# A two-layer attention trunk in one core: the identity matrix made by GpSimd instead of loaded, and a new order of instructions

## The chip, the core and the metric

The kernel runs on one core of a Trainium2 chip. The core has a TensorE for matmuls (PE in the profile, its weight loads PEld), a VectorE (DVE), a ScalarE (ACT), a GpSimd (POOL) and a SyncE (SP); transfers are issued here by SP and by ScalarE and carried out by 16 DMA engines. The metric is the device time of one execution in microseconds. Before the change it is 305.41 us (median of three runs, 304.03 to 306.15).

## The reference

A sequence of 256 tokens of width 1024 passes through two layers. Each layer normalises x, applies a shift and a scale that come from a conditioning vector c, runs its attention mixer, and adds the result to x through a gate from c. A last normalisation follows. Cut to what matters:

```python
c_act = silu(c)
for layer in range(2):
    shift, scale, gate = split(c_act @ w_ada[layer] + b_ada[layer], 3)
    h = rms_norm(x, norm_g[layer]) * (1 + scale) + shift
    if layer == 0:   # projection 1024 -> 2840, two head groups:
        # A: 8 query heads on 1 key head, window 128, with a sink per head
        # B: 8 query heads on 2 key heads: compressed keys, selected blocks and a window, gated
        y = even_mixer(h, w_in_even, w_out_even, ...)
    else:            # projection 1024 -> 4096, 16 heads, blocks of 256 keys
        y = odd_mixer(h, w_in_odd, w_out_odd, ...)
    x = x + gate * y
return rms_norm(x, final_g)

# compressed keys and values of B: windows of 32 tokens every 16, as one row each
k_cmp = gelu((windows(k) + pe_k) @ w1_k) @ w2_k      # w1: 2048 x 256
```

All of it is in float32. The attention outputs are multiplied by the silu of a part of the projection before the output projection.

## The kernel before

**Planned order.** The kernel's Python code first records every operation (class Plan, record) with what it depends on; then Plan.issue (line 262) makes the real calls in the order of a table of about 2900 numbers, ORDER. All operations therefore carry the line of that call, L269, in the profile, and are told apart by their tiles. Each engine executes its own operations in this order, one behind the other: an operation that has to wait holds back all that stands behind it on its engine. The same goes for the DMAs that SP or ScalarE issues. A second table, FLIP, names the copies, scalings and affine maps that go to the other one of ScalarE and DVE than the code says.

**Arithmetic.** A float32 product is made of three matmuls (mm3): high part by high part, high by low, low by high. Weights arrive in one of five raw buffers of 1 MB each (raw0 to raw4); ScalarE casts them to the high part whi, DVE subtracts to get the low part wlo. hhi and hlo are the same two parts of the layer's input h, transposed; ghi and glo those of the attention's output.

**The opening.** TensorE begins with filler matmuls on a constant matrix ones, whose results are not used (into ps_m and ps_o). ScalarE's queue loads norm_g and b_ada (into rows), the table tbl_a (into ta, 128 x 160: columns 0 to 127 the identity matrix ident, 128 to 159 a selection matrix sel) and c (into crow, 8 x 128). SP's queue loads x (two halves of 128 tokens, xs), the first weights of w_in_even (raw) and those of w_ada. small_c transposes crow on TensorE with ident into ps_pt, and makes silu(c) from it (ACT tiny, DVE tiny, DVE cz). For each half of x, ScalarE squares and sums (ACT t<-xs), GpSimd takes the inverse root (r, with a power by expo), DVE and ScalarE scale (t<-xs,r), TensorE transposes (ps_s<-ta,t and ps_pj<-ta,t), and copies bring the result to xT, which lies in bigA.

**Shift and scale of layer 0.** They are made for groups of the eight row blocks g of the weights: START says for one block, then two, two, two and one. For each group, w_ada lands in tiles that are used later for other things (qT, gate, oT, kTb, t, called room in start_ada), and start_sums multiplies with cz on TensorE (ps_m<-qT,cz, ps_m<-oT,cz, ...) and partly on DVE (acc). blk and asb fold the sums, shs holds the result, and start_prep makes hhi and hlo of block g by ScalarE and DVE. start_mm then adds block g to seven accumulators.

**After that** follow rotary embeddings, transposes and attention A, the compression (compress_mlp: weights cmp_w1_k and cmp_w1_v in raw buffers, multiplied directly, ps_m<-raw,t), attention B, the output projection (ps_s<-whi,ghi), and the change of layer: out of the sums of squares in parts comes the inverse root, t<-xs,parts scales, TensorE transposes, t<-ps_pj,shs applies scale and shift, hhi and hlo are made, and the second layer's projection begins (ps_pj<-whi,hhi). The second layer's shift, scale and gates are made on DVE along the way (acc<-raw,cz,acc, summed over partitions by a matmul with ones). The last product is normalised and stored.

Transposes everywhere multiply by ident. sel has two readers: the compression, and selbc, a copy of one column of sel that GpSimd spreads over 128 columns.

## Time and profile before

| what | value |
|---|---|
| runs, median | 305.41 us (304.03, 305.41, 306.15) |
| the profiled execution | 303.29 us |
| its span, first to last instruction | 301.4 us |
| TensorE busy | 290.8 us (96%) |
| DVE busy | 258.1 us (86%) |
| ScalarE busy | 198.5 us (66%) |
| GpSimd busy | 11.4 us (4%) |
| DMA | 71.83 MB, mean 238 GB/s |

The profile shows one execution on the chip. Times of its rows are microseconds from the start of the span. A row of the timeline has start, length, engine, line, operation, output and inputs; in brackets stands the idle time of the engine before it and what ended that. Matmul ends are modelled, so the distance between the starts of two matmuls says more of their price than their length does. A wait for several things is put down to the one that came last by the profile. What the profiled execution takes outside its span is 303.29 - 301.4 = 1.9 us.

### The profile page before, as it was taken

The numbers are of one execution on the slowest core, as the hardware profiler recorded it, in microseconds if no ns is written. First come the engines' busy times: TensorE is split into PE (matmuls) and PEld (weight loads), VectorE is DVE, ScalarE is ACT, GpSimd is POOL, SyncE is SP. The second block draws the span as 40 slices with busy tenths as digits, with TensorE's granted clock in tenths as the row PEclk, the third lists the DMA queues.
The fourth block names the chain that finished last, engine by engine and source line by source line (L and its number), as shares of the span: only waits on it lengthen the run. The fifth ranks groups of instructions, "written<-read, shape, count | busy, mean of one in ns | idle before, by whom it ended". The sixth has DMA issues, their size and how long they took to land.

```text
span 301.4 us, 6166 instructions
## 1 busy us (share of the span) xinstructions
PE 290.8 (96%) x2268; PEld 250.4 (83%) x2268; DVE 258.1 (86%) x648; ACT 198.5 (66%) x506; POOL 11.4 (4%) x36
## 2 busy tenths in 40 slices
PE   7999999999999999999998999999999999999990
PEld 6888888897698888777877799999889989887890
DVE  0479988999999999999999867998788999987873
ACT  1655646796999989996459764377376467782620
POOL 1300000002000000000010000000000000000021
PEclk9999999999999999999999999999999999999998
DMA  7999999975989774389995947099782973103103
GB/s 244 368 385 369 397 350 377 385 240 170 377 265 340 266 256 157 113 285 372 292 299 186 315 134 272 4 306 383 222 255 93 311 246 100 44 3 138 71 2 139
DMA packets 60751, 71.83 MB, mean 238 GB/s; under 512 B 2761, under 2 KB 52401, under 8 KB 60721
## 3 DMA queue, kind: packets, MB, share of 16 engines
q1 hardware_dynamic: 60176, 70.92, 69.1%
q10 hardware_dynamic: 544, 0.51, 0.5%
q8 instruction: 18, 0.29, 0.4%
q14 instruction: 13, 0.10, 0.1%
HBM read 70.38 MB, written 1.05 MB: 237 GB/s over the span
## 4 chain that ended last, share of the span: by engine, by line
PE 89%; DVE 3%; ACT 2%; issue 2%; DMA 2%; POOL 1%; ACTq 0%; POOLq 0%; DVEq 0%
PE ps_pj L269 56%; PE ps_s L269 10%; PE ps_pt L269 8%; PE ps_o L269 8%; PE ps_m L269 7%; DMA crow<-in_c_dram 2%; DVE t L269 1%; ACT t L269 1%; DVE xs L269 1%; ACT whi L269 1%; ACTq L269 0%; POOL parts L269 0%; DVE acc L269 0%; DVE wlo L269 0%; POOLq L1393 0%
## 5 line engine op out<-in xcount | busy, mean ns | idle before, releaser
L269 ACT CAST whi<-raw 128x512 fp32r<-128x512 f32 (+2 forms) x108 | 72.0, 691 | 32.3 <-PE ps_pj L269 17.9
L269 PE MATMUL ps_pj<-hhi,whi 128*128 128x256 f32 x256 | 74.0, 296 | 0.0
L269 PE MATMUL ps_pj<-hlo,whi 128*128 128x256 f32 x256 | 72.8, 290 | 0.0
L269 DVE TENSOR_TENSOR wlo<-raw,whi 128x512 fp32r<-128x512 f32 (+2 forms) x92 | 70.8, 792 | 2.2 <-ACT whi L269 1.9
L269 PE MATMUL ps_pj<-hhi,wlo 128*128 128x256 f32 x256 | 70.7, 287 | 0.0
L269 PEld LDWEIGHTS ps_pj<-hhi,whi 128*128 128x128 f32 x256 | 47.8, 188 | 2.8 <-issue 2.0
L269 PEld LDWEIGHTS ps_pj<-hlo,whi 128*128 128x128 f32 x256 | 47.9, 188 | 1.9 <-issue 1.7
L269 PEld LDWEIGHTS ps_pj<-hhi,wlo 128*128 128x128 f32 x256 | 47.3, 188 | 0.7 <-issue 0.6
L269 DVE SCALAR_TENSOR_TENSOR acc<-raw,cz,acc 128x512 f32<-128x512 f32 x56 | 41.6, 744 | 0.3
L269 ACT ACTIVATE sm<-sm,mn 128x256 f32<-128x256 f32 (+1 forms) x58 | 26.0, 450 | 7.3 <-DVE mn L269 7.3
L269 PE MATMUL ps_pj<-whi,hhi 128*128 128x512 f32 (+2 forms) x72 | 25.8, 377 | 0.5 <-ACT hhi L269 0.5
L269 PE MATMUL ps_pj<-wlo,hhi 128*128 128x512 f32 (+2 forms) x72 | 25.9, 377 | 0.0
L269 PE MATMUL ps_pj<-whi,hlo 128*128 128x512 f32 (+2 forms) x72 | 25.3, 372 | 0.0
L269 DVE SCALAR_TENSOR_TENSOR wlo<-raw,whi 128x512 fp32r<-128x512 f32 x32 | 21.2, 686 | 3.7 <-ACT whi L269 3.6
L269 PE MATMUL ps_pj<-wlo,ghi 128*128 128x512 f32 (+1 forms) x56 | 20.6, 371 | 0.0
L269 PE MATMUL ps_pj<-whi,glo 128*128 128x512 f32 (+1 forms) x56 | 20.6, 370 | 0.0
L269 PE MATMUL ps_pj<-whi,ghi 128*128 128x512 f32 (+1 forms) x56 | 20.5, 368 | 0.0
L269 ACT ACTIVATE sm<-sm,rc 128x256 f32<-128x256 f32 (+1 forms) x44 | 18.7, 453 | 2.0 <-DVE rc L269 2.0
L269 PE MATMUL ps_pt<-ta,sm 128*128 128x128 f32 x87 | 17.8, 274 | 0.0
L269 DVE TENSOR_TENSOR t<-ps_pj,tb 128x512 f32<-128x512 f32 (+2 forms) x22 | 12.1, 588 | 4.4 <-PE ps_pj L269 4.4
L269 PEld LDWEIGHTS ps_pj<-whi,hhi 128*128 128x128 f32 x72 | 13.4, 188 | 2.8 <-ACT hhi L269 1.2
L269 ACT ACTIVATE whi<-raw 128x512 fp32r<-128x512 f32 x16 | 9.7, 627 | 8.8 <-PE ps_pj L269 5.3
(241 smaller groups left out, 610.1 us busy)
## 6 DMA issues: line engine op xcount, KB each, us to landing
raw<-in_w_ada_dram SPq DMA_DIRECT2D x32, 512.0 KB, 5.0
raw<-in_w_in_odd_dram SPq DMA_DIRECT2D x16, 1024.0 KB, 7.0
raw<-in_w_in_even_dram SPq DMA_DIRECT2D x8, 652.0 KB, 7.0
raw<-in_w_in_even_dram SPq DMA_DIRECT2D x5, 1024.0 KB, 7.0
raw<-in_w_out_even_dram SPq DMA_DIRECT2D x4, 1024.0 KB, 5.2
raw<-in_w_out_odd_dram SPq DMA_DIRECT2D x4, 1024.0 KB, 6.5
qT<-in_w_ada_dram SPq DMA_DIRECT2D x12, 256.0 KB, 6.2
t<-in_w_ada_dram SPq DMA_DIRECT2D x8, 256.0 KB, 6.5
```

Of the source, the lines that this page charges most:

```text
L269: self.ops.append(dict(key=eng.key, deps=deps, fn=lambda: getattr(real, name)(*args, **kw)))
```

## The change

The table tbl_a shrinks to 128 x 32, the selection matrix alone. It is loaded by SP behind the tables of the rotary embedding. ident is a tile of its own, which GpSimd fills with ones and then cuts to the diagonal, as its first work in the kernel. The copy selbc goes, as do functions that no call reached with the settings of before (ada_tile, ada_rows) and the settings themselves (SS_ON, G0_ON, G1_ON); the matmuls stay the same in number and shape. Both tables, ORDER and FLIP, are new.

```diff
-    ta = const([P, 160], "ta")
+    ident = const([P, P], "ident")
+    sel = const([P, 32], "sel")
+    G.memset(ident, 1.0)
+    G.affine_select(out=ident, in_=ident, compare_op=ALU.is_equal, fill=0.0, base=0, pattern=[[-1, P]], channel_multiplier=1)
...
-    A.dma_start(ta, tbl_a)
...
-    ident = ta[:, 0:128]
-    sel = ta[:, 128:160]
...
-    selbc = const([P, P], "selbc")
-    G.tensor_copy(selbc, sel[:, 0:1].to_broadcast([P, P]))
...
     Y.dma_start(tb, tbl_b[:, :1056])
+    Y.dma_start(sel, tbl_a)
...
-    a = np.zeros((P, 160), np.float32)
-    a[:, :128] = np.eye(P)
+    a = np.zeros((P, 32), np.float32)
...
-            a[32 * q + m, 128 + m] = 1.0
+            a[32 * q + m, m] = 1.0
...
 ORDER = [int(i) for i in """
-93 4 5 3 6 0 8 20 21 22 23 24 25 26 27 28 29 50 54 55 56 57 30 58 31 32 33 34 35 53 1 62 59 97 2 52 1010 1015 40
+7 0 2 4 1 9 21 22 23 24 25 26 27 28 29 30 54 31 32 33 34 6 3 41 5 93 97 96 92 94 55 95 77 56 100 98 62 78 79 35
...
```

By FLIP, DVE now makes more of the opening's copies to bigA (and fewer of asb), and in the attention stage fewer copies of kTb and scalings of sm and more of the copies pT; the count of ScalarE's operations is the same.

GpSimd's instructions begin, behind four small constants, with the memset of ident, a reload of its library, the select, then the memset of expo and the root r; the memset of cz (288 columns), which was the first, stands behind the roots. The library reload stood between the memset of expo and the first operation of r before.

In the opening, this is ScalarE's instruction stream before (tiny is the silu of c; t_88 and t_90 take the squares of the two halves of x):

```order
L269 DMA rows<-in_norm_g_dram 16x128
L269 DMA rows<-in_b_ada_dram 48x128
L269 DMA ta<-in_tbl_a_dram 128x160
L269 DMA crow<-in_c_dram 8x128
L269 ACT_TABLE_LOAD
L269 ACTIVATE tiny_86<-ps_pt_85 128x8
L269 ACTIVATE t_88,r_87<-xs 128x1024
L269 CAST whi_110<-raw_101 128x152
```

And after:

```order
L266 DMA crow<-in_c_dram 8x128
L266 DMA rows<-in_b_ada_dram 48x128
L266 DMA rows<-in_norm_g_dram 16x128
L266 ACT_TABLE_LOAD
L266 ACTIVATE tiny_86<-ps_pt_85 128x8
L266 ACTIVATE t_90,r_87<-xs 128x1024
L266 ACTIVATE t_88,r_87<-xs 128x1024
L266 CAST whi_109<-raw_101 128x512
L266 CAST whi_110<-raw_101 128x512
```

The load of crow has moved from the last of ScalarE's four to the first of its three, that of ta is gone, and the two squares follow each other without a cast between.

On TensorE, these rows lead to the first projection matmul of the opening before (they follow the sums ps_m<-qT,cz; ps_m<-oT,cz are the same kind of sums for the next two row blocks; whi and hhi belong to the projection; x8 counts like rows in a run):

```order
L269 MATMUL ps_pj_95<-ta,t_91 128x128 x2
L269 MATMUL ps_s_93<-ta,t_89 128x128 x2
L269 MATMUL ps_pj_95<-ta,t_91 128x128
L269 MATMUL ps_pj_94<-ta,t_91 128x128
L269 MATMUL ps_m_67<-blk,asb_107 128x2
L269 MATMUL ps_o_69<-ones 128x128
L269 MATMUL ps_s_93<-ta,t_89 128x128
L269 MATMUL ps_o_69<-ones 128x128
L269 MATMUL ps_pj_95<-ta,t_91 128x128
L269 MATMUL ps_m_67<-oT,cz 32x128 x8
L269 MATMUL ps_pj_96<-whi_109,hhi 128x512
```

And after:

```order
L266 MATMUL ps_pj_95<-ident,t_91 128x128
L266 MATMUL ps_pj_94<-ident,t_91 128x128
L266 MATMUL ps_pj_95<-ident,t_91 128x128 x2
L266 MATMUL ps_pj_94<-ident,t_91 128x128
L266 MATMUL ps_m_68<-blk,asb_107 128x2
L266 MATMUL ps_s_93<-ident,t_89 128x128 x2
L266 MATMUL ps_o_70<-ones 128x128
L266 MATMUL ps_pj_95<-ident,t_91 128x128
L266 MATMUL ps_o_70<-ones 128x128 x2
L266 MATMUL ps_s_93<-ident,t_89 128x128
L266 MATMUL ps_pj_96<-whi_109,hhi 128x512
```

The eight matmuls ps_m<-oT,cz no longer stand ahead of the first projection matmul (ps_pj_96<-whi_109,hhi); they come behind 13 matmuls of the projection. On SP, the two loads of xs are now the first two DMAs; before, they were the second and the fourth, with tiles of w_ada and of w_in_even ahead of them.

At the change of layer, TensorE's stream before is (ps_s<-whi,ghi is the output projection of layer 0, ps_pj_96 and ps_o the transposes of the first tokens, ps_pj_94 the projection of layer 1):

```order
L269 MATMUL ps_s_93<-whi_110,ghi 128x512
L269 MATMUL ps_s_93<-wlo_114,ghi 128x512
L269 MATMUL ps_s_93<-whi_110,glo 128x512
L269 MATMUL ps_pj_96<-ta,t_88 128x128 x4
L269 MATMUL ps_o_69<-ta,t_88 128x128 x4
L269 MATMUL ps_pj_94<-whi_111,hhi 128x512
L269 MATMUL ps_pj_94<-wlo_115,hhi 128x512
L269 MATMUL ps_pj_94<-whi_111,hlo 128x512
```

And after:

```order
L266 MATMUL ps_s_93<-whi_110,glo 128x512
L266 MATMUL ps_pj_96<-ident,t_88 128x128 x3
L266 MATMUL ps_s_93<-whi_110,ghi 128x512
L266 MATMUL ps_pj_96<-ident,t_88 128x128
L266 MATMUL ps_s_93<-wlo_114,ghi 128x512
L266 MATMUL ps_s_93<-whi_110,glo 128x512
L266 MATMUL ps_o_70<-ident,t_88 128x128 x3
L266 MATMUL ps_pj_94<-whi_111,hhi 128x512
L266 MATMUL ps_pj_94<-wlo_115,hhi 128x512
L266 MATMUL ps_o_70<-ident,t_88 128x128
L266 MATMUL ps_pj_94<-whi_111,hlo 128x512
```

Three matmuls of the output projection now stand between the transposes of ps_pj_96 and those of ps_o, and the first two matmuls of the next projection ahead of the last transpose. On ScalarE, the cast that stood between the two t<-xs,parts has moved away from there.

For the compression, SP's stream before holds these loads (raw_101 to raw_105 are raw0 to raw4; cmp_w_k and cmp_w_v with 128x8x256 are the 1 MB weights):

```order
L269 DMA tb<-in_tbl_b_dram 128x1056
L269 DMA raw_104<-in_w_in_even_dram 128x8x256
L269 DMA raw_101<-in_w_in_even_dram 128x8x256
L269 DMA raw_105<-in_w_in_even_dram 128x8x256
L269 DMA raw_102<-in_cmp_w_k_dram 128x8x256
L269 DMA raw_103<-in_cmp_w_k_dram 128x8x256
L269 DMA raw_104<-in_cmp_w_v_dram 128x8x256
L269 DMA w2v<-in_cmp_w_v_dram 128x2x64
L269 DMA raw_105<-in_cmp_w_v_dram 128x8x256
L269 DMA raw_102<-in_w_in_even_dram 128x8x256
L269 DMA w2k<-in_cmp_w_k_dram 128x2x64
```

And after:

```order
L266 DMA tb<-in_tbl_b_dram 128x1056
L266 DMA raw_105<-in_w_in_even_dram 128x8x256
L266 DMA snk<-in_a_sinks_dram 128x8
L266 DMA w2v<-in_cmp_w_v_dram 128x2x64
L266 DMA w2k<-in_cmp_w_k_dram 128x2x64
L266 DMA raw_101<-in_w_in_even_dram 128x8x256
L266 DMA sel<-in_tbl_a_dram 128x32
L266 DMA raw_104<-in_cmp_w_v_dram 128x8x256
L266 DMA raw_102<-in_cmp_w_k_dram 128x8x256
L266 DMA raw_103<-in_cmp_w_k_dram 128x8x256
L266 DMA raw_105<-in_cmp_w_v_dram 128x8x256
```

Both loads of cmp_w_k stood ahead of the first load of cmp_w_v; now they stand behind it, and it waits for raw_104, which the load of the projection weights three rows above the piece (raw_104<-in_w_in_even) fills. The tiles w2v and w2k have moved ahead, and the load of sel is new.

## The prediction

> **What bounds the kernel now.** The page was read first: span, busy shares, the DMA row of the 40 slices and the head of the chain of waits.

> ```profile
> span 301.4 us, 6166 instructions
> PE 290.8 (96%) x2268; PEld 250.4 (83%) x2268; DVE 258.1 (86%) x648; ACT 198.5 (66%) x506; POOL 11.4 (4%) x36
> DMA  7999999975989774389995947099782973103103
> PE 89%; DVE 3%; ACT 2%; issue 2%; DMA 2%; POOL 1%; ACTq 0%; POOLq 0%; DVEq 0%
> ```

> TensorE is busy for 290.8 of 301.4 us and carries 89% of the chain. An order can therefore only win back 301.4 - 290.8 = 10.6 us. The table of windows says where they lie (columns: window, its length, then busy time and count of PE, PEld, DVE, ACT, POOL, granted clock, DMA share, GB/s).

> ```profile
> 0.00:16.50 16.50, 13.88 (x129) 12.58 (x129) 4.93 (x16) 7.29 (x14) 4.24 (x24) 1.00 0.93 313
> 16.50:57.00 40.50, 40.50 (x294) 34.16 (x287) 36.42 (x79) 23.16 (x54) 0.00 (x0) 1.00 1.07 377
> 70.00:148.00 78.00, 78.00 (x653) 62.49 (x653) 75.82 (x236) 67.13 (x202) 0.99 (x2) 1.00 0.79 267
> 148.00:160.00 12.00, 10.90 (x50) 8.27 (x49) 11.86 (x23) 7.42 (x16) 1.96 (x4) 1.00 0.95 325
> ...
> 288.00:301.40 13.40, 6.51 (x52) 6.18 (x50) 7.32 (x16) 1.64 (x4) 2.28 (x3) 0.92 0.21 79
> ```

> Idle TensorE time stands in three places: 2.6 us in the opening (much of whose busy time is filler matmuls on ones), 1.1 us at the change of layer (148 to 160) and 6.9 us in the tail after 288; these make up the whole 10.6. From 16.5 to 57 TensorE has no gap, but the DMA engines have none either (share 1.07, 377 GB/s): that stage has two bounds at once. The timeline shows what sets the opening (start, us, engine, operation, and in brackets the idle time before it with what ended it).

> ```profile
> 1.64 4.28 PE L269 MATMUL ps_o<-ones 128*128 128x128 f32 x20
> 2.23 0.43 SPq L269 DMA_DIRECT2D xs<-in_x_dram  x1
> ...
> 4.94 1.29 SPq L269 DMA_DIRECT2D qT<-in_w_ada_dram  x2
> 7.08 0.19 PE L269 MATMUL ps_pt<-ta,crow 8*128 8x8 f32 x1 [1.16 <-DMA crow<-in_c_dram]
> 7.39 1.05 ACT L269 ACTIVATE t<-xs 128x1024 f32<-128x1024 f32 x1
> ...
> 9.82 0.49 DVE L269 TENSOR_SCALAR t<-xs,r 128x512 f32<-128x512 f32 x1 [1.54 <-POOL blk L269]
> ...
> 12.22 0.48 DVE L269 TENSOR_SCALAR t<-xs,r 128x512 f32<-128x512 f32 x1
> ...
> 13.29 1.08 PE L269 MATMUL ps_m<-qT,cz 128*32 128x128 f32 x32
> ...
> 15.99 0.64 PE L269 MATMUL ps_m<-oT,cz 128*32 128x128 f32 x16
> ...
> 16.57 0.50 PE L269 MATMUL ps_pj<-whi,hhi 128*128 128x512 f32 x1
> ```

> crow, fourth on ScalarE's queue, comes late. Behind it follow the squares of x, the normalised rows t, their transposes, ps_m<-qT and the first projection matmul at 16.57.

> **The opening, part by part.** Landing times stand in the answers on DMA issues (KB, us to landing; asked for the moments of issue 0.7, 2.2 and 5.5 us).

> ```profile
> rows<-in_norm_g_dram ACTq DMA_DIRECT2D x1, 8.0 KB, 2.6
> ```
> ```profile
> xs<-in_x_dram SPq DMA_DIRECT2D x1, 512.0 KB, 5.7
> ```
> ```profile
> qT<-in_w_ada_dram SPq DMA_DIRECT2D x1, 256.0 KB, 6.5
> ```

> Issued first, as norm_g is now, crow lands at about 0.74 + 2.6 = 3.3 us. The filler matmuls ahead of it end at 1.64 + 4.28 = 5.9, so the crow transpose moves from 7.08 to 5.9. The identity must be there by then too. It is free of ta, which GpSimd's copy of it (row below) saw at 6.66, and now costs a 128x128 memset and a select on GpSimd, started at about 0.7. No row shows a select. The nearest are a memset and a 128x128 copy there:

> ```profile
> 0.73 0.34 POOL L269 MEMSET cz<- 128x288 f32 x1 [0.29 <-POOLq L1383]
> 6.66 0.29 POOL L269 COPY selbc<-ta 128x128 f32<-128x128 f32 x1 [5.59 <-DMA ta<-in_tbl_a_dram]
> ```

> About 0.3 + 0.3 makes it ready at 1.4; four times as much is still hidden by the filler. Removing the copy selbc is worth nothing, GpSimd being idle.

> Both halves of x now lead SP's queue. The second landed at 2.23 + 5.7 = 7.9; without 448 KB (qT, raw) and ta's 80 KB ahead, at 377 GB/s, it lands 1.4 earlier, at 6.5. ScalarE's first square starts at 6.2 instead of 7.39, so the first normalised half comes at about 9.0 (was 9.82) and the last at about 11.1 (12.22). The values cz, which DVE now writes behind these, stand at 11.3. The last qT tile landed at about 5.5 + 6.5 = 12.0 and lacks ta's 80 KB ahead, 0.2 us: 11.8. So ps_m<-qT starts at 11.8 instead of 13.29, 1.5 earlier, and the oT group, now behind 13 projection matmuls, takes its cadence of 0.57 out of the path: the first projection matmul comes 2.1 earlier, at about 14.5.

> Not all of that is kept. The second row group has to wait for its weights:

> ```profile
> 20.32 0.62 ACT L269 CAST whi<-raw 128x512 fp32r<-128x512 f32 x1
> 21.79 0.60 ACT L269 ACTIVATE hhi<-bigA,shs 128x256 fp32r<-128x256 f32 x1 [0.85 <-DVE shs L269]
> ```
> ```profile
> 22.74 0.63 PE L269 MATMUL ps_s<-whi,hhi 128*128 128x512 f32 x2
> ```

> From 16.57 to 22.74 TensorE has 6.2 us of work; started at 14.5 it ends at 20.7. The weights arrive by a full DMA queue that has only ta's 0.2 us less to carry, so the cast stands at 20.1; hhi, ordered behind it, comes at 20.7 instead of 21.79. Kept: 1.1. Bounds: 0.2 if the DMA queue alone sets the pace up to 57 us, 2.1 if it nowhere does. I take 1.1 by these ACT rows.

> **The change of layer.**

> ```profile
> 156.94 0.40 PE L269 MATMUL ps_s<-whi,glo 128*128 128x512 f32 x1
> 157.49 0.66 PE L269 MATMUL ps_pj<-ta,t 128*128 128x128 f32 x4 [0.15 <-ACT t L269]
> 158.62 0.66 PE L269 MATMUL ps_o<-ta,t 128*128 128x128 f32 x4 [0.47 <-ACT t L269]
> 159.75 0.49 PE L269 MATMUL ps_pj<-whi,hhi 128*128 128x512 f32 x1 [0.47 <-ACT hhi L269]
> ```
> ```profile
> 156.71 0.72 ACT L269 ACTIVATE t<-xs,parts 128x512 f32<-128x512 f32 x1 [1.66 <-POOL parts L269]
> 157.34 0.60 ACT L269 CAST whi<-raw 128x512 fp32r<-128x512 f32 x1
> 157.85 0.72 ACT L269 ACTIVATE t<-xs,parts 128x512 f32<-128x512 f32 x1
> ```

> TensorE runs dry three times. Three 512-column matmuls, 0.23 us apart in the dense stretch, now lie between the transposes: 3 x 0.23 = 0.7 out of the waits. The cast between the two t is gone from there (0.5 us), which lets the second set come sooner. Bounds: 0, if the chain from parts to hhi still ends last, and the 1.6 us of all three gaps (hole from 157.2 to 157.5 and two of 0.64 before 158.62 and 159.75). I take 0.7.

> **Weights of the compression.** The two loads of cmp_w1_k now stand on SP behind cmp_w1_v, whose buffer is raw3.

> ```profile
> 50.17 5.14 SPq L269 DMA_DIRECT2D raw<-in_cmp_w_k_dram  x2
> 60.88 0.37 SPq L269 DMA_DIRECT2D raw<-in_cmp_w_v_dram  x1
> ```
> ```profile
> raw<-in_cmp_w_v_dram SPq DMA_DIRECT2D x1, 1024.0 KB, 6.1
> ```
> ```profile
> 71.12 1.93 PE L269 MATMUL ps_m<-raw,t 128*32 128x256 f32 x32
> ```

> Before, they were issued from 50.17. Now they wait for raw3, free at 60.88, or 59.8 with 1.1 from the opening; the first load lands 6.1 later, each further MB takes 1.05 / 377 = 2.8 us, so the third lands at 59.8 + 6.1 + 5.6 = 71.5. TensorE wants it at 71.12 - 1.1 plus about 1.6 us of work now ahead (21 rows of its order, an estimate from matmuls of 0.12 to 0.23), 71.6. That is a draw; I charge 0.2 (bounds 0 and 6.8, rival D). Behind a late load nothing on TensorE can pass.

> **The rest.** The small table sel (16 KB) is loaded beside the others long before its use, cost nothing. Moving work between ScalarE and DVE nets about one microsecond more on DVE in the opening (of its idle 11) and some tenths less between 70 and 148, where DVE idles only 78.0 - 75.82 = 2.2; TensorE covers both. The tail's order is the same, 0.

> Sum: -1.1 - 0.7 + 0.2 + 0 = -1.6. The profiled execution took 303.29 us, so 301.7 there. The median of the runs, 305.41, lies 2.1 above it; in its frame: 303.8.

> **Rivals.** A measurement of this kernel can tell about 1% (3.05 us) from no change.
> B, the DMA queue eats the opening: hhi arrives with the weights in every row group, 0.2 kept of 1.1, and the change of layer gives 0.7: 305.41 - 0.9 + 0.2 = 304.7. For it the share of 1.07; against it that the same stretch has TensorE at 40.50 of 40.50.
> C, more than forecast: the opening keeps 2.1, the three gaps give 1.6: 305.41 - 3.7 = 301.7. For it, that order changed all over and DVE's tight stretch gets lighter; against it, that both need their upper bounds.
> D, slower: the three compression loads are served one after another, 6.1 us each, from 60.88: the third lands at 79.2, TensorE wanting it at 72.4 in that frame; 6.8 us of wait less 1.8 gained: 310.4. Below 2 us of wait it only undoes the gain; beyond 4.9 us it costs 1%. For it, the order on SP; against it, that three weight loads issued within 45.5 to 46.7 landed in a median of 9.0, not 18:

> ```profile
> raw<-in_w_in_even_dram SPq DMA_DIRECT2D x3, 1024.0 KB, 9.0
> ```

> E, the identity comes late. GpSimd's library reload stands before the select now and stood before r's operations:

> ```profile
> 8.62 0.22 POOL L269 TENSOR_SCALAR r<-r 128x1 f32<-128x1 f32 x1 [1.08 <-ACT t L269]
> ```

> The row waited 1.08 us and is put down to ScalarE's square, so the reload cost at most that much there, so identity by 2.5 and covered. If the select nevertheless came only after 7 us, crow's transpose would stay at about 7.1, the opening would gain nothing, and the sum is -0.7 + 0.2: 304.9. [...]

> **How the numbers follow.** Forecast 0.45 (own range 302.6 to 304.9), B 0.15, C 0.22, D 0.12, E 0.06. Faster by over 1% (below 302.36): C but for 0.02, and 0.05 of the forecast: 0.25. Slower by over 1% (above 308.46): D but for 0.01: 0.11, and 0.01 for its like elsewhere: 0.12. The same: 0.63. The range 301.0 to 307.5 leaves out D and some 0.08 of C.

> **What would show it.** crow's transpose near 5.9 and the first projection matmul near 14.5; the second group's at 21.6 (22.7 says B); gaps around the layer's transposes summing to 0.9; ps_m<-raw with a wait of less than 1 us on the load of cmp_w1_k (over 3 says D); the tail after its last projection as long as before. A stall of TensorE in the middle of a layer that was dense before would make the sum wrong altogether.

## The result, and the profile after

The changed kernel takes 301.79 us (median of four runs, 301.49 to 301.87) against 305.74 us (303.29 is its profiled execution; four timed runs of 304.03 to 306.15). The ratio is 0.9879, with a 95% interval from 0.984 to 0.9919: about 1.2% faster. The two profiled executions, 303.29 and 301.74 us, lie only 1.55 us apart, while the medians lie 3.95 apart. That difference between the two distances is what the experiments had to explain.

The page of the changed kernel, its first two rows and the head of its chain:

```profile
span 299.9 us, 6179 instructions
PE 290.6 (97%) x2268; PEld 250.4 (83%) x2268; DVE 258.9 (86%) x647; ACT 198.1 (66%) x507; POOL 11.7 (4%) x37
PE 89%; DMA 6%; DVE 2%; issue 1%; POOL 0%; ACT 0%; POOLq 0%; ACTq 0%; DVEq 0%
```

TensorE does the same work in a span that is 1.5 us shorter. Its windows after the change (columns as before):

```profile
14.50:57.00 42.50, 42.43 (x308) 35.68 (x306) 37.44 (x81) 24.91 (x61) 0.00 (x0) 1.00 1.06 370
...
70.00:148.00 78.00, 78.00 (x647) 61.94 (x646) 75.24 (x239) 67.28 (x203) 1.00 (x2) 1.00 0.82 274
148.00:160.00 12.00, 11.31 (x51) 8.47 (x50) 11.75 (x25) 8.29 (x19) 2.56 (x4) 1.00 0.69 236
...
288.00:299.90 11.90, 4.95 (x42) 4.75 (x41) 6.53 (x16) 1.63 (x4) 2.27 (x3) 0.93 0.24 90
```

The tail idles 11.90 - 4.95 = 6.95 us as before, and the attention stage is as dense as before. The opening, from the timeline:

```profile
1.08 0.29 POOL L266 TENSOR_SCALAR_AFFINE_SELECT ident<-ident 128x128 f32<-128x128 f32 x1
1.71 3.79 PE L266 MATMUL ps_o<-ones 128*128 128x128 f32 x20
5.43 0.22 PE L266 MATMUL ps_pt<-ident,crow 8*128 8x8 f32 x1
5.59 1.60 PE L266 MATMUL ps_o<-ones 128*128 128x128 f32 x12
7.65 2.17 PE L266 MATMUL ps_m<-ones 128*128 128x128 f32 x18
7.90 0.49 DVE L266 TENSOR_SCALAR t<-xs,r 128x512 f32<-128x512 f32 x1 [0.24 <-POOL r L266]
11.46 1.08 PE L266 MATMUL ps_m<-qT,cz 128*32 128x128 f32 x32
14.30 0.49 PE L266 MATMUL ps_pj<-whi,hhi 128*128 128x512 f32 x1
...
21.29 0.62 PE L266 MATMUL ps_pj<-whi,hhi 128*128 128x512 f32 x2
```

The identity is ready at 1.37 us, the transpose of crow waits for nothing, and the first projection matmul starts at 14.30 instead of 16.57. The first of the second row block starts at 21.29 instead of 22.74: 1.45 of the 2.27 us are kept.

### The profile page after: what moved, and what is told of

The parts are those of the page before. It is cut to its first block, busy times and chain, and to the rows that moved or that the text cites. A ratio compares the mean times of both kernels' runs of the same rounds, so it can differ in the third digit from the quotient of the medians.

```text
span 299.9 us, 6179 instructions
## 1 busy us (share of the span) xinstructions
PE 290.6 (97%) x2268; PEld 250.4 (83%) x2268; DVE 258.9 (86%) x647; ACT 198.1 (66%) x507; POOL 11.7 (4%) x37
## 3 DMA queue, kind: packets, MB, share of 16 engines
HBM read 70.31 MB, written 1.05 MB: 238 GB/s over the span
## 4 chain that ended last, share of the span: by engine, by line
PE 89%; DMA 6%; DVE 2%; issue 1%; POOL 0%; ACT 0%; POOLq 0%; ACTq 0%; DVEq 0%
PE ps_pj L266 56%; PE ps_s L266 13%; PE ps_pt L266 7%; PE ps_o L266 7%; PE ps_m L266 6%; DMA kTb<-in_w_ada_dram 2%; DMA qT<-in_w_ada_dram 2%; DMA rows<-in_b_ada_dram 2%; DVE t L266 1%; DVE xs L266 1%; POOL parts L266 0%; ACT t L266 0%; POOLq L1338 0%; ACTq L266 0%; DVE hlo L266 0%
## 5 line engine op out<-in xcount | busy, mean ns | idle before, releaser
L266 ACT CAST whi<-raw 128x512 fp32r<-128x512 f32 (+2 forms) x108 | 71.2, 689 | 24.4 <-PE ps_pj L266 13.1
L266 PE MATMUL ps_pj<-hlo,whi 128*128 128x256 f32 x256 | 72.4, 292 | 0.0
L266 PE MATMUL ps_pj<-wlo,hhi 128*128 128x512 f32 (+2 forms) x72 | 26.6, 379 | 0.0
L266 PE MATMUL ps_pj<-whi,hlo 128*128 128x512 f32 (+2 forms) x72 | 26.1, 375 | 0.1
L266 ACT ACTIVATE sm<-sm,rc 128x128 f32<-128x128 f32 (+1 forms) x48 | 20.5, 445 | 3.0 <-DVE rc L266 2.9
L266 PE MATMUL ps_pj<-whi,glo 128*128 128x512 f32 (+1 forms) x56 | 20.1, 367 | 0.0
L266 PE MATMUL ps_pt<-ident,sm 128*128 128x128 f32 x87 | 18.3, 273 | 0.0
L266 ACT ACTIVATE t<-xs 128x512 f32<-128x512 f32 (+2 forms) x7 | 5.0, 718 | 16.0 <-DVE xs L266 16.0
L266 PEld LDWEIGHTS ps_pj<-whi,hlo 128*128 128x128 f32 x72 | 13.4, 189 | 2.4 <-DVE hlo L266 0.4
## 6 DMA issues: line engine op xcount, KB each, us to landing
raw<-in_w_ada_dram SPq DMA_DIRECT2D x32, 512.0 KB, 6.0
raw<-in_w_in_odd_dram SPq DMA_DIRECT2D x16, 1024.0 KB, 5.9
raw<-in_w_in_even_dram SPq DMA_DIRECT2D x5, 1024.0 KB, 8.3
raw<-in_w_out_even_dram SPq DMA_DIRECT2D x4, 1024.0 KB, 5.8
raw<-in_w_out_odd_dram SPq DMA_DIRECT2D x4, 1024.0 KB, 6.0
qT<-in_w_ada_dram SPq DMA_DIRECT2D x12, 256.0 KB, 5.9
t<-in_w_ada_dram SPq DMA_DIRECT2D x8, 256.0 KB, 6.7
```

Of the source, the lines that this page charges most:

```text
L266: self.ops.append(dict(key=eng.key, deps=deps, fn=lambda: getattr(real, name)(*args, **kw)))
```

## The experiments

Orders were edited by moving entries of the table; the diffs below show the rows that move on one engine. "Before" is always a set of runs of the kernel before made beside them on the same chip. One row of fillers in a diff is two instructions in the profile: x10 here is x20 there, and a time per filler is that of one instruction.

**1. The kernel before once more.** No edit.

> The kernel before, unchanged, timed many times and profiled once more. The profiled executions of before and after lie 1.55 us apart, the medians of their runs 3.6 to 3.9. Theory V: the order of before has a place that sometimes stalls, so its times here spread over 2 to 3 us (303.3 to 306.2), and a new profile of a run above 305 shows an extra stall of TensorE of about 2 us at one place. Rival N: the spread belongs to the chip or the moment and not to the kernel; then its times here lie within 0.5 us of each other, and a new profile has the same gaps as the old one.

Measured: 305.21 us, twelve runs from 302.8 to 306.54; the kernel before itself, eighteen runs beside it, 306.03 (302.6 to 306.83). So the spread belongs to the kernel, and the profile that the forecast was built on is one of its shortest executions. The new profile is of an execution of 306.2 us, span 304.4. Its opening, first TensorE and GpSimd rows:

```profile
1.64 4.48 PE L269 MATMUL ps_o<-ones 128*128 128x128 f32 x20
7.90 0.27 PE L269 MATMUL ps_pt<-ta,crow 8*128 8x8 f32 x1 [1.79 <-DMA ta<-in_tbl_a_dram]
7.91 0.29 POOL L269 COPY selbc<-ta 128x128 f32<-128x128 f32 x1 [6.84 <-DMA ta<-in_tbl_a_dram]
9.12 2.93 PE L269 MATMUL ps_o<-ones 128*128 128x128 f32 x12
13.55 2.14 PE L269 MATMUL ps_m<-ones 128*128 128x128 f32 x16
16.16 1.08 PE L269 MATMUL ps_m<-qT,cz 128*32 128x128 f32 x32
```

And two of the same rows in the profile of before that the forecast used:

```profile
7.95 1.60 PE L269 MATMUL ps_o<-ones 128*128 128x128 f32 x12
10.86 1.95 PE L269 MATMUL ps_m<-ones 128*128 128x128 f32 x16
```

Two things differ. The table landed late, so that TensorE idled 1.79 us ahead of the transpose of crow instead of 1.16 and began it 0.82 later. And the twelve fillers behind it took 2.93 us instead of 1.60: TensorE ran them at 0.21 us each, where all but the first took 0.11 in the other execution. The trace's record of the granted TensorE clock has it full from 13.93 us on here, and from 5.60 us on there, before that execution's wait. Fillers stand ahead of the transposes of x in TensorE's stream, so at half the rate they are the path: ps_m<-qT starts at 16.16 instead of 13.29, 2.87 us later, and the spans differ by 3.0. Theory V held, with its place in the opening; rival N fell. What made the rate late was still open: the experiments from 5 on ask that.

**2. The identity alone.** Order and engines of before.

```diff
 GpSimd
+MEMSET ident 128x128
+AFFINE_SELECT ident<-ident 128x128
 MEMSET cz 128x288
-COPY selbc<-ta 128x128
 ScalarE
 DMA rows<-in_norm_g_dram 16x128
 DMA rows<-in_b_ada_dram 48x128
-DMA ta<-in_tbl_a_dram 128x160
 DMA crow<-in_c_dram 8x128
```

> The order and the engines of before; only the identity is made by GpSimd, the small table is loaded behind the tables of the rotary embedding, selbc is gone. Theory O (the order does it): crow is still issued behind norm_g and b_ada, at about 1.75 instead of 2.23, so it lands near 6.4, its transpose moves from 7.08 to about 6.4, the second half of x still lands near 7.7: the first projection matmul comes 0.3 to 0.7 us earlier and the time falls by 0.2 to 0.6 us. Rival I (the identity does it): the time falls by 1.3 us or more.

Measured: 302.61 us (seven runs, 301.98 to 302.92), ratio to before 0.9913 (0.9877 to 0.9948). By the medians rival I is right: 3.4 us. By the profiles theory O is: its span is 300.9, 0.5 below that of the first profile of before. Both numbers are one fact. The edit takes about 0.5 us from a lucky execution of before, and it takes away the unlucky ones: TensorE goes from the fillers to the transpose of crow without a wait, and in this profile the half rate ends at 7.23 us.

**3. The order alone**, identity loaded.

```diff
 ScalarE
 DMA crow<-in_c_dram 8x128
+DMA ta<-in_tbl_a_dram 128x160
 DMA rows<-in_b_ada_dram 48x128
 GpSimd
-MEMSET ident 128x128
-AFFINE_SELECT ident<-ident 128x128
...
+COPY selbc<-ta 128x128
```

(against the kernel after)

> The order and the engines of after, but the identity is still loaded with its table, second on ScalarE's queue behind crow, and selbc is still copied. Theory O: the table lands near 5.5 to 6.5, so the crow transpose is at 5.9 to 6.6 instead of 5.43, and the kernel is within 0.3 to 0.9 us of after: 302.0 to 302.7. Rival I: it stays within 0.5 us of before, since TensorE waits for the table as long as before.

Measured: 302.15 us (six runs, 302.0 to 302.57), ratio 0.9898 (0.9857 to 0.994). Theory O's number. The identity and the order each do nearly all of it without the other: 3.4 and 3.9 us below the runs of before, where both together give 4.1 (experiment 4). Their gains do not add, since both shorten the same wait: ahead of the transpose of crow, none is left in the profile of experiment 2 and 0.79 us in that of experiment 3.

**4. The new opening, the old rest.** ORDER is that of after up to the last matmul of the eight row blocks, that of before behind it.

> The identity made by GpSimd; order and engines of after up to the last matmul of the eight row blocks (about 57 us), order and engines of before from there on. The sum of the forecast gives the opening 1.1 (profiles: 1.3 to 1.4 by the time TensorE reaches the same amount of work), the change of layer 0.7 (0.2 in the profile). Theory O: it gains 1.3 to 1.5 us of span on the profiled execution of before and leaves 0.2 to 0.5 to after. If the runs of before are longer because of a stall behind 57 us (theory V, late place), its times spread as those of before; if the place is in the opening, its times lie within 0.5 us of each other.

Measured: 301.90 us (six runs, 301.46 to 302.12), ratio 0.9885 (0.9847 to 0.9923); span of its profile 300.3. The order behind 57 us is worth no more than a few tenths: 0.4 us between this profile and that of after, nothing between the medians. And the spread is gone with the opening alone.

**5. Crow and table first.** The kernel before with one edit on ScalarE's queue.

```diff
+DMA crow<-in_c_dram 8x128
+DMA ta<-in_tbl_a_dram 128x160
+DMA rows<-in_b_ada_dram 48x128
 DMA rows<-in_norm_g_dram 16x128
-DMA rows<-in_b_ada_dram 48x128
-DMA ta<-in_tbl_a_dram 128x160
-DMA crow<-in_c_dram 8x128
```

> The kernel before with one edit: ScalarE issues the load of crow first and that of the table second, ahead of b_ada and norm_g; identity still loaded, order and engines of before. Theory G (a gap in TensorE's filler work keeps its rate at half): crow and table land near 6, the wait of 1.2 to 1.8 us goes, the fillers reach 0.11 us each before 8.5 us, and the times become tight at 302.3 to 303.3, 2.5 to 3.5 us below the median of before. Rival L (only the late start counts): the gain is what the transpose comes earlier, 1 to 2 us, and the spread of before stays.

Measured: 302.84 us, ratio 0.9952 (0.9929 to 0.9975) to before at 304.73. Not tight: seven of twelve runs lie from 302.14 to 302.85, as theory G has it, and five from 303.72 to 304.48. The profile fell on a run of 304 us (span 302.1) and shows why. The wait has not gone, it has moved to the next transpose, whose rows now come last:

```profile
5.47 0.20 PE L280 MATMUL ps_pt<-ta,crow 8*128 8x8 f32 x1 [0.26 <-DMA ta<-in_tbl_a_dram]
7.54 0.34 PE L280 MATMUL ps_pt<-ta,rows 64*128 64x64 f32 x1 [1.46 <-DMA rows<-in_norm_g_dram]
7.81 2.93 PE L280 MATMUL ps_o<-ones 128*128 128x128 f32 x12
```

The windows of this profile show the clock that was granted around the gap (the second number from the right of the row's end is the DMA share, the one before it the granted clock):

```profile
6.00:8.00 2.00, 0.54 (x3) 0.37 (x3) 0.33 (x3) 1.12 (x3) 1.08 (x6) 0.88 0.99 336
8.00:11.00 3.00, 3.00 (x15) 3.00 (x16) 1.12 (x3) 2.67 (x5) 1.44 (x8) 0.51 1.07 345
11.00:12.00 1.00, 1.00 (x11) 1.00 (x11) 0.84 (x2) 0.84 (x3) 0.29 (x5) 1.00 1.11 377
```

TensorE had been at its full rate from 4.1 us, idled, and was granted 0.51 of its clock from 8 to 11 us. The fillers' 0.21 us, against 0.11 at full clock, is that half clock. (The column reads 1.00 up to the first change on record, which is the change to full clock at 13.93 us in experiment 1; the half rate ahead of it shows there in the fillers alone.) The record of this profile changes in steps of 3.41 us: full from 4.09, half from 7.51, full again from 10.92. The stretch from 4.09 to 7.51 is the one with the gaps of 0.26 and 1.46 us.

Every timed run has its mean granted clock on record, and a stretch of 3.41 us at half clock lowers it by about 0.006 (1.7 of 302 us). The five long runs of this experiment stand at 0.987 to 0.989, the seven short ones at 0.992 to 0.997. Of the 58 runs of before made beside the experiments, 39 stand below 0.99, none of them under 303.86 us; of the runs of the kernel after and of experiments 2, 3, 4 and 8, none does.

The moment from which the record has the clock full for the first time differs from execution to execution: 4.26 us in experiment 3, 4.63 and 6.38 in two profiles of the kernel after, 5.60 and 13.93 in two of the kernel before. Gaps of 1.46 us (this one), 1.79, 2.15 and 1.65 (experiments 1, 9 and 12) went with 3.4, 6.0, 6.4 and 3.4 us of half clock behind them.

**6. Fillers into the gap.** The kernel before; on TensorE:

```diff
 MATMUL ps_o_69<-ones 128x128 x10
+MATMUL ps_o_69<-ones 128x128 x5
 MATMUL ps_pt_85<-ta,crow 128x8
-MATMUL ps_o_69<-ones 128x128
 MATMUL ps_pt_85<-ta,rows 128x64
-MATMUL ps_o_69<-ones 128x128 x6
+MATMUL ps_o_69<-ones 128x128 x2
```

> The kernel before with one edit: five of the filler matmuls that stood behind the transpose of crow stand ahead of it, so that TensorE is busy until about 8 us; loads, order of all else and engines of before. The transpose cannot come earlier, it comes up to 1 us later than in the first profile (8.0 against 7.08). Theory G: without the gap the fillers change from 0.21 to 0.11 us each at about 7 to 8.5 us in every run, and although the chain starts no earlier the times are tight at 302.8 to 304, 2 to 3 us below the median of before. Rival L: the times stay at or above those of before (306), with the same spread.

Measured: 303.52 us, ratio 0.9965 (0.9948 to 0.9983) to before at 304.73. Eleven of thirteen runs lie from 302.83 to 303.93, where theory G put them; nothing is loaded earlier and no work is left out, so rival L falls. The edit also takes ten filler instructions out of the path behind the transpose, 1.1 us at 0.11 each, but its runs are no shorter than the shortest of before on this chip (302.96 to 303.47): what it takes away is the long runs. Two runs lie at 306.91 and 307.39, and the profile is of such a one: the table landed at 8.41 us, later than the fillers reach. The clock had been full from 6.58 us; gaps of 0.94 and 0.46 us fell into that stretch, and the half clock began at 10.00 and lasted to 16.82 us, with another gap in it. These two runs alone stand below 0.99 in their mean clock (0.986).

```profile
8.46 0.22 PE L280 MATMUL ps_pt<-ta,crow 8*128 8x8 f32 x1 [0.94 <-DMA ta<-in_tbl_a_dram]
11.77 1.11 PE L280 MATMUL ps_s<-ta,t 128*128 128x128 f32 x4 [0.91 <-DVE t L280]
12.67 3.62 PE L280 MATMUL ps_m<-ones 128*128 128x128 f32 x16
```
```profile
10.00:17.00 7.00, 6.09 (x30) 5.71 (x28) 2.14 (x5) 3.94 (x8) 2.81 (x14) 0.51 1.11 379
```

**7. A longer gap.** The opposite move.

```diff
-MATMUL ps_o_69<-ones 128x128 x10
+MATMUL ps_o_69<-ones 128x128 x5
 MATMUL ps_pt_85<-ta,crow 128x8
-MATMUL ps_o_69<-ones 128x128
+MATMUL ps_o_69<-ones 128x128 x6
```

> The kernel before with the opposite edit: five of the ten filler matmuls ahead of the transpose of crow stand behind it, so that TensorE is idle from about 3.8 us until the table and crow are there. Theory G: the change from 0.21 to 0.11 us per filler comes only after 10 to 14 us in every run; with five more fillers still ahead of ps_m<-qT, the times are 306 to 308 and the low runs of before (302.6) are gone. Rival L: the fillers hide behind the same wait, and times and spread are as those of before.

Measured: 306.81 us (six runs, 305.58 to 307.12), ratio 1.0072 (1.0043 to 1.01): theory G, and no run as low as those of before. Ten filler instructions more behind the transpose are 1.1 us of work at full rate and 2.1 at half; the median rose by 2.1. The profile (of 305.58, the shortest) has the wait and the slow fillers behind it; the full rate comes back at 10.92 us:

```profile
7.76 0.24 PE L280 MATMUL ps_pt<-ta,crow 8*128 8x8 f32 x1 [3.78 <-DMA crow<-in_c_dram]
7.93 2.93 PE L280 MATMUL ps_o<-ones 128*128 128x128 f32 x12
```

**8 and 11. Two small moves in the kernel after.** Three fillers from ahead of the transpose of crow to behind it, and on GpSimd:

```diff
 TENSOR_SCALAR r_87<-r_87 128x1
-MEMSET blk 128x8
-MEMSET blk 64x1
 TENSOR_TENSOR r_87<-r_87,expo 128x1
+MEMSET blk 128x8
+MEMSET blk 64x1
```

> The kernel after with two small moves: three of the filler matmuls ahead of the transpose of crow stand behind it (5.43 becomes about 4.2), and the two memsets of blk that stood between GpSimd's second scaling and second power of r stand behind the power. If the chain of crow, squares and roots sets the opening, the second root is ready 0.3 to 0.6 us earlier and the time falls by 0.1 to 0.4 us, to 301.4 to 301.7; if the second half of x (landed at 6.42) or the weights of the second row block set it, nothing changes. A gap that opens ahead of the transpose would show as a late change of the fillers' rate and a loss of 1 to 3 us.

> The same kernel as in the run with the two small moves (three fillers behind the transpose of crow, the memsets of blk behind the second power), now beside the kernel after on one chip: 0.1 to 0.4 us below it if the moves are worth anything, equal within 0.1 if its 301.49 came from the other chip.

Measured: 301.49 us (301.37 to 301.7), ratio 0.9902 (0.9875 to 0.993), and on the second chip 301.57 (301.36 to 301.63), ratio 0.9886 (0.9855 to 0.9916), beside 301.89 for the kernel after (next). The runs of the two do not overlap there: the two moves together take 0.3 us off the kernel after, and which of them does it was not tried. No gap opened, as the transpose still waits for nothing.

**9. A gap in the kernel after.**

```diff
 ScalarE
-DMA crow<-in_c_dram 8x128
-DMA rows<-in_b_ada_dram 48x128
 DMA rows<-in_norm_g_dram 16x128
+DMA rows<-in_b_ada_dram 48x128
+DMA crow<-in_c_dram 8x128
 TensorE
-MATMUL ps_o_70<-ones 128x128 x10
+MATMUL ps_o_70<-ones 128x128 x5
 MATMUL ps_pt_85<-ident,crow 128x8
-MATMUL ps_o_70<-ones 128x128 x6
+MATMUL ps_o_70<-ones 128x128 x11
```

> The kernel after, with a gap put into its filler work: crow is loaded behind norm_g and b_ada (as before the change), and five of the ten fillers ahead of its transpose stand behind it, so that TensorE idles from about 3.7 to 6.5 us. The identity is still made by GpSimd. Theory G: the gap keeps the fillers at 0.21 us until 8 us or later, and the time rises by 2 to 3.5 us, to 303.8 to 305.3. Rival I (the loaded table is what cost, whatever TensorE does meanwhile): only the later transpose counts, about 1.1 us of which a good half is kept, 302.3 to 302.9.

Measured: 304.47 us (twelve runs, 303.98 to 305.33), 2.6 above the unchanged kernel after on the same chip (below), and with the kernel before (305.0) within the interval: ratio 0.9982 (0.9958 to 1.0006). Theory G. The edit gives back 2.6 of the 3.1 us that the change gains on this chip, with the identity made and the order otherwise new. The later start is not what costs: the transpose begins at 6.20 us, against 6.11 in the profile of experiment 10. The ten filler instructions more behind it are 1.1 us of work at full rate; at least 1.5 us are left for the half clock, which lasts to 12.55 us here:

```profile
6.20 0.24 PE L277 MATMUL ps_pt<-ident,crow 8*128 8x8 f32 x1 [2.15 <-DMA crow<-in_c_dram]
6.37 5.06 PE L277 MATMUL ps_o<-ones 128*128 128x128 f32 x22
```

**10. The kernel after once more**, beside the others of this chip.

> The kernel after, unchanged, beside the others on one chip: 301.5 to 302.0 by its four runs so far, and tight; theory G expects no run above 302.5, since nothing in its filler work waits. A new profile shows the same gaps at the change of layer (about 1.4 us in all).

Measured: 301.89 us (six runs, 301.84 to 302.24), ratio 0.99 (0.987 to 0.9931): tight, as expected, with the same idle time at the change of layer (0.68 us from 148 to 160). In its profile the clock became full at 6.38 us, not at 4.63 as in the first one, and the first projection matmul starts at 15.02 instead of 14.30; the span is only 0.2 us longer.

**12. The smallest edit.** Order of before, identity made, crow first.

```diff
 ScalarE
-DMA rows<-in_norm_g_dram 16x128
-DMA rows<-in_b_ada_dram 48x128
 DMA crow<-in_c_dram 8x128
+DMA rows<-in_b_ada_dram 48x128
+DMA rows<-in_norm_g_dram 16x128
```

(against experiment 2)

> The smallest edit that removes both waits: order and engines of before, identity made by GpSimd, and crow issued first by ScalarE; rows (b_ada, norm_g) behind it. Theory G: with the identity made alone the fillers already ran without a gap (302.6), so crow first adds at most the 0.3 us by which the transpose comes earlier, if the rows transpose does not wait in its place: 302.2 to 302.6. If rows come so late that TensorE idles over 1 us ahead of its transpose, part of the runs are 1 to 2 us longer, as with crow first and the table loaded.

Measured: 302.30 us (six runs, 301.77 to 303.91), ratio 0.9915 (0.9883 to 0.9948): five runs up to 302.41, and one at 303.91, which the profile caught. It is the second case of the expectation: rows come last, the gap is ahead of their transpose, and the clock is 0.50 from 8 to 11 us.

```profile
7.53 0.26 PE L277 MATMUL ps_pt<-ident,rows 64*128 64x64 f32 x1 [1.65 <-DMA rows<-in_norm_g_dram]
7.72 2.93 PE L277 MATMUL ps_o<-ones 128*128 128x128 f32 x12
```
```profile
8.00:11.00 3.00, 3.00 (x15) 3.00 (x16) 0.71 (x3) 2.38 (x5) 0.95 (x6) 0.50 1.07 344
```

The order of the kernel after loads rows last too, but has six fillers between the two transposes, where the order of before has one: with 1.60 us of work there, the rows are in place when their turn comes. By these rows, that is the part of the new order that the smallest edit lacks; it was not tried by itself.

## Why the prediction was right, and where not

The time, 301.79, lies in the range, on its fast side. The likeliest case, no change that can be told (303.8), is not what happened; the measured ratio lies beyond the 1% bound, its interval on both sides of it.

The sum itself came out: forecast -1.6 us against the profiled execution's own time, measured 301.74 - 303.29 = -1.55. That it agrees so closely is luck, since the terms miss in both directions. Its terms:

- **Opening, 1.1 forecast, about 1.45 measured** at the second row block (1.18 in the second profile of the kernel after, where it starts at 21.56). Step by step: crow's transpose at 5.43 (forecast 5.9), identity ready at 1.37 (1.4), first normalised half at 7.90 (9.0), ps_m<-qT at 11.46 (11.8), first projection matmul at 14.30 (14.5), second block at 21.29 (21.6). The transpose came before 5.9 because the clock became full at 4.63 us in this execution; in the other it was at 6.11. The cause given for the loss is not what held TensorE up. ScalarE's cast did wait for the weights, and hhi was ready at 20.34 + 0.60 = 20.94:

```profile
19.82 0.62 ACT L266 CAST whi<-raw 128x512 fp32r<-128x512 f32 x1 [0.44 <-DMA raw<-in_w_in_even_dram]
20.34 0.60 ACT L266 ACTIVATE hhi<-bigA,shs 128x256 fp32r<-128x256 f32 x1
```

But TensorE had other work until 21.29 and shows no wait for hhi there. From the first projection matmul to the second block it took 6.17 us before and 6.99 after. The forecast took the sums ps_m<-oT, 0.57 us, out of the path ahead of this stretch and did not add them to it, though they now stand in it; besides, a weight load of the sums that follow waited for kTb. By TensorE's own work the forecast would have been 14.5 + 6.2 + 0.57 = 21.3; that the 21.6 came out close is luck too.

```profile
18.21 0.25 PEld L266 LDWEIGHTS ps_m<-kTb,cz 128*32 128x32 f32 x10 [0.34 <-DMA kTb<-in_w_ada_dram]
```

- **Change of layer, 0.7 forecast, 0.2 to 0.4 measured.** By the windows the idle time from 148 to 160 falls from 1.10 to 0.69; taken from the starts of the matmuls, the gaps fall from 1.6 us (0.32, 0.64, 0.64) to 1.4 (0.18, 0.76, 0.24, 0.21). The matmuls do fill the gap ahead of ps_o, but the chain from parts to hhi and hlo still ends last, which was the condition of the lower bound: the wait for hhi is 0.59 instead of 0.47, and a new one, for hlo, follows it.

```profile
156.62 0.49 PE L266 MATMUL ps_o<-ident,t 128*128 128x128 f32 x3
157.70 0.50 PE L266 MATMUL ps_pj<-whi,hhi 128*128 128x512 f32 x1 [0.59 <-ACT hhi L266]
158.63 0.19 PEld L266 LDWEIGHTS ps_pj<-whi,hlo 128*128 128x128 f32 x1 [0.44 <-DVE hlo L266]
```

- **Weights of the compression, +0.2 forecast, 0 measured.** The buffer came free earlier than forecast (the first load was issued at 57.92, not 59.8), and the later load of cmp_w1_k landed at 69.86, 1.5 us ahead of its reader:

```profile
71.38 1.93 PE L266 MATMUL ps_m<-raw,t 128*32 128x256 f32 x32
```

**The step that failed** is the last one of the sum: the median of the runs "lies 2.1 above it; in its frame: 303.8". The 2.1 us between the profiled execution of before and its median was carried over to the kernel after as if it were outside the kernel. It was the cost of the half clock in most executions of before (39 of 58 with a mean below 0.99), which went with the wait ahead of crow's transpose, and the change removes it. The wait itself was in the forecast (1.16 us, from the very row), priced as a start that comes 1.2 us earlier, and not as a gap behind which the fillers can cost twice as much (0.21 us each instead of 0.11 in experiment 1). In the profile of experiment 1 ps_m<-qT came 2.87 us later, 0.82 of it by the later start, which leaves about 2 us for the half clock; the edit of experiment 9 cost 2.6 us, at most 1.1 of it for the moved fillers. Had the offset not been carried over, the forecast would have been 301.7.

**The rivals.** B (DMA eats the opening) did not happen. C gives the time that was measured, but not by its mechanism: the opening kept 1.45 and not 2.1, and the change of layer did not give 1.6. D did not happen: the last of the three loads landed 11.9 us after the first was issued, where the forecast had 11.7 and D 18.3. (In D's sum, the 72.4 us at which TensorE wants the weights should read 71.12 + 1.6 = 72.7, which makes its wait 6.5 us.) E did not happen: the select ran at 1.08 us, 0.08 after the end of the memset ahead of it, so the library reload between them cost no more than that. The select after 7 us that E supposed is in no profile: where the identity is made, the transpose of crow that reads it started at 5.43 us (the kernel after), 6.20, 6.11 and 5.23 (experiments 9, 10 and 12).

Left open: the rule by which a gap leads to half clock. The stretches of 3.41 us on record say part of it. Two that began at full clock with a gap of 1.16 us (the first profile of before, from 5.60) or 0.79 (experiment 3, from 4.26) were followed by full clock; four with gaps of 1.40 us or more in all (experiments 5, 6, 7 and 12) were followed by half clock. Between 1.16 and 1.40 us, and on what ends the half clock, there are too few cases. The table of before landed between 6.61 and 8.41 us in four profiles with the same queues; why it varied was not tried, nor was a kernel without fillers.

## What to carry to other kernels

Where a kernel's runs spread by a per cent and its profile lies at the low end, profile it again before a change is priced: the difference between two executions of one program shows what is fragile, and a change can be worth more than any one profile holds. In an opening like this one, a TensorE that waits for a small load may pay twice, once for the wait and once for a halved clock behind it (1.46 us and then 3.4 us at half clock in experiment 5), and filler work that was free becomes the path where it stands ahead of the rest of the stream (twelve fillers took 2.93 us instead of 1.60 in experiment 1); put the smallest, first-needed loads ahead on their queue, make on an idle engine what can be made, and spread the filler so that every transpose finds its data.
